# u as two more seven-product pairs in a hybrid decoder block on one core

## The chip, the cores and the metric

The kernel runs on one core of a Trainium2 chip. The metric is the device time of one execution in microseconds (us). The core has five engines with instruction queues of their own: PE (TensorE, matrix products into PSUM), DVE (VectorE), ACT (ScalarE), POOL (GpSimd, here small vector work and a queue of DMAs) and SP (SyncE, here only a queue of DMAs). Every queue runs in order: an instruction that waits for a semaphore holds back all that stand behind it on that engine.

## What is computed

The whole is one decoder block on 1024 tokens of width 1024 in float32. The part that matters here is the first half:

```python
h = _rmsnorm(x, g_mix_pre[l])
proj = jnp.einsum('bsd,de->bse', h, w_in[l]) + b_in[l]
u_pool, q, k, v, gates = jnp.split(proj, IN_SPLITS, axis=-1)   # 512, 512, 128, 128, 2048 columns
y_pool = _multiscale_pool(u_pool, w_pool[l], pool_scale[l])
...
y_attn = _sliding_window_sink_attention(q, k, v, attn_sinks[l])
g = jax.nn.sigmoid(gates)
g_pool, g_attn = g[..., :D_MODEL], g[..., D_MODEL:]
merged = (g_pool * jnp.einsum('bsc,cd->bsd', y_pool, w_branch_pool[l])
          + g_attn * jnp.einsum('bsc,cd->bsd', y_attn, w_branch_attn[l]))
```

The output projection, the residuals, the norms and the squared-ReLU MLP follow. Their code is not touched.

## The kernel before

Operands of float32 products are held as a high and a low part (`split`, L99: ACT casts to the high part, L101 or L103, then DVE subtracts it for the low part, L104). A product takes three matmul passes, high x high, high x low, low x high (`PASSES`). A matmul is 128 rows by 128 columns of weights against 512 columns of tokens.

**Stages of the first half.** First come q, k and v of the first four token tiles. Then the attention (L788 to L868) runs over eight tiles n of 128 tokens: transposes of the probabilities (`attend_t`, L396), masking (`attend_own`), the exponentials of the next tile (`softmax_exp`), their scaling, the product with v (`attend_v`, L420), scores of the tile after next (`score`), q and k of a later one (`post_qkv`). This is a long chain of ACT and DVE work, and PE would idle in it, so a generator `others` (L676) hands out other PE work in portions: `fill(t)` takes about t us from it. Its work is q, k, v of the later tiles, then per group gi of 128 columns u (`u_half`, L638: 24 matmuls for each half of the tokens) and the product of the pool weight with the branch weight (`wb_mm`, L659). `between` holds the operand splits that belong to it, which run at the middle of a portion.

The gates follow: 2048 columns as eight pairs of 256 columns. `Pairs` (L472) computes a 2 x 2 block product with seven half-size products of 12 matmuls each (4 blocks of the inner dimension, three passes) in place of eight, by sums of weight blocks and of input blocks. The products 1, 2, 3 read the plain inputs (`B11`, `B21`, `B22`), 4 to 7 read sums of inputs (`T1` to `T4`), which `build_gate` (L766) makes from x, loaded once more. Products 1 and 2 of all eight pairs run first (`first`, `second`), with the input sums built beside them. Their result `f0` stays in SBUF for six pairs and is spilled to DRAM for two. Then a loop over the pairs p does the rest: weights loaded (`load`), their sums and splits (`operand`), products 6, 4 and 3 of the pair before, 5, 7. The results are scaled with the norm (`rb`), pass a sigmoid and go to DRAM (`gate_close*`).

Last, the attention's output is fetched (`load_attn`, L933: two loads per quarter, added by DVE at L942, then split) and eight branches follow, each with 24 matmuls for the attention half (`branch`, L981). Among them stand the four pooling steps (`pool_part`, L990), which load u, add shifted copies and split.

**Order.** Inside `tc.manual_schedule` blocks the program's own order holds for the named engines. Elsewhere a scheduler orders the instructions at build time. Tiles come from pools with a fixed number of buffers (`st` 3, `wp` 6, `ga` 6, `yy` 4, `xp` 16, `gp` 17; PSUM: 2 x 2 banks `sc` and 4 `mm` in the attention, 4 `at` and 4 `mm` after), and a new tile waits until its buffer is free.

Of the kernel before, what the change touches and what calls it, by code (L numbers as in the profile page):

```python
# [14 lines left out]
P = 128  # L15
# [35 lines left out]
def block_kernel(ctx: ExitStack, tc, xt, x, consts, vecs, sinks, b_qkv, g_post, g_mlp, g_mlp_post,  # L51
# [344 lines left out]
    def attend_t(n):  # L396

        s8 = scores.pop(n)
        pt = [at("s4", 4, [NH, P], F32R) for _ in range(2)]
        bs = bank("sc", [2, 4, P])  # L400
        for kv in range(2):
            for m in range(4):
                pe.transpose(bs[:, kv, m], s8[:, kv, m], ident)  # L403
# [68 lines left out]
    class Pairs:  # L472
# [15 lines left out]
        def operand(self, p, i):  # L488
# [20 lines left out]
            self.w[p, i] = t  # L509
# [7 lines left out]
        def mm(self, b, p, i, kts=range(4), after=False):  # L517
            w, xo = self.w[p, i], self.X[OPERAND[i]]
            for kt in kts:
                for j, (wh, xh) in enumerate(PASSES):  # L520
                    x_ = xo[kt][xh] if isinstance(xo[kt], tuple) else xo[kt][:, xh, :]
                    pe.matmul(b, w[:, wh, kt, :], x_, start=not after and kt == 0 and j == 0,  # L522
                              stop=kt == 3 and j == 2, skip_group_check=after)
# [84 lines left out]
    between, hurry, due = ([], []), [False], ([], [])  # L608
# [8 lines left out]
    def load_u(gi):  # L617
        ws = stage([NK, P])
        nc.sync.dma_start(ws, w_u[gi])

        def parts():
            wu[gi] = wslot([NK, P]), wslot([NK, P])
            split(*wu[gi], ws)
        between[1].append(parts)

    def load_wb(gi):
# [9 lines left out]
        between[0].append(parts)  # L636

    def u_half(gi, th):  # L638

        if th == 0:  # L640
            ut[gi] = ga_.tile([P, S], F32, tag="ga", name=nm("u"))
        (whi, wlo), u = wu[gi], ut[gi]
        sl = slice(th * 512, (th + 1) * 512)
        b = bank("mm")

        mms = [(k, xh, 0) for k in range(NK) for xh in range(2)] + [(k, 0, 1) for k in range(NK)]
        for j, (k, xh, h) in enumerate(mms):
            pe.matmul(b, (whi, wlo)[h][:, k, :], xr(k, xh, th), start=j == 0, stop=j == len(mms) - 1)  # L648
            if j == 7 and hurry[0]:
                due[th].append(lambda: flush(between[th]))  # L650
            elif j == 7:
                flush(between[th])
            if j % 2:
                yield 2 * 0.227
        dve.tensor_tensor(u[:, sl], b, rb[:, sl], ALU.mult)
        if th == 1:
            nc.sync.dma_start(u_dram[gi], u)
# [16 lines left out]
    ut, wpts = {}, []  # L674

    def others():  # L676
        for n in range(4, NT):
            bq[n] = bank("mm")
            for k in range(NK):
                mm_q(n, k, bq[n])  # L680
                if n == NT - 1 and k == 3:
                    flush(between[1])
# [3 lines left out]
            if n == 5:  # L686
                load_u(3)
# [7 lines left out]
        for gi in (3, 2, 1, 0):  # L695
            load_wb(gi)
            if gi:
                load_u(gi - 1)
            yield from u_half(gi, 0)
            yield from u_half(gi, 1)  # L700
            yield from wb_mm(gi)
# [13 lines left out]
    def pool_in(gi, u, place):  # L715
# [4 lines left out]
        while step < w:  # L720
# [3 lines left out]
            src, step = t, 2 * step  # L724
        dve.scalar_tensor_tensor(u[:, w - 1:], src[:, w - 1:], 1.0 / w, u[:, w - 1:], ALU.mult, ALU.subtract)
        dve.tensor_tensor(src[:, :w - 1], src[:, :w - 1], cst[:, C_CNT:C_CNT + w - 1], ALU.mult)
        dve.tensor_tensor(u[:, :w - 1], src[:, :w - 1], u[:, :w - 1], ALU.subtract)

# [4 lines left out]
    def gate_first(f, b):  # L733
        dve.tensor_tensor(f, b, rb[:, :512], ALU.mult)

    def gate_close(m, f):
        act.activation(f, f, AF.Sigmoid, bias=vec[:, V_BG + m:V_BG + m + 1])
        nc.scalar.dma_start(z_dram[m], f)

    def gate_close0(m, f):  # L740
        dve.tensor_tensor(f[:, 512:], f[:, 512:], rb[:, 512:], ALU.mult)
        gate_close(m, f)

    def gate_close1(m, f):
        dve.tensor_tensor(f, f, rb, ALU.mult)
        gate_close(m, f)

    def gate_close_third(m, f, b):
        dve.tensor_tensor(f[:, 512:], f[:, 512:], rb[:, 512:], ALU.mult)
        dve.tensor_tensor(f[:, :512], b, rb[:, :512], ALU.mult)  # L750
# [5 lines left out]
    gt = Pairs(w_g, ar, gate_result, gate_first, gate_close0, gate_close1, gate_close_third)  # L756
# [9 lines left out]
    def build_gate(kt, place):  # L766

        ab = raw_x.pop(kt)
        act.activation(ab[0], ab[0], AF.Identity, scale=vec[:, V_G + kt:V_G + kt + 1])
        gb = vec[:, V_G + 4 + kt:V_G + 5 + kt]  # L770
        a0, a1, b0, b1 = (t[:, th * 512:(th + 1) * 512] for t in ab for th in range(2))
# [4 lines left out]
        yield  # L776
        for name, src in (("T2", b1), ("T1", a0), ("T3", a1), ("T4", b0)):
            t = place()
            split(t[:, 0, :], t[:, 1, :], src)
            gt.X[name][kt] = t  # L780
        yield
# [6 lines left out]
    with tc.manual_schedule(engines={mybir.EngineType.PE, mybir.EngineType.DVE, mybir.EngineType.Activation}):  # L788
# [39 lines left out]
        for n in range(NT):  # L828
# [3 lines left out]
            if n + 1 < NT:  # L832
                softmax_exp(n + 1, range(8))
            if n + 1 < NT:
                softmax_scale(n + 1)
                fill(5.0 if n == 1 else 4.4)
# [3 lines left out]
            else:  # L840
                fill(4.0)
                gt.prepare(0)
# [3 lines left out]
            if n == 6:  # L846
                load_x(0, lambda: at("qkv", 3, [S]))
# [9 lines left out]
            if n + 3 < NT:  # L857
                post_qkv(n + 3)
            if n + 2 < NT:
                softmax_max(n + 2)  # L860
        gt.prepare(1)
# [3 lines left out]
        gt.prepare(2)  # L865
        load_x(1, lambda: ga_.tile([P, S], F32, tag="ga", name=nm("xr")))
        for _ in build_gate(0, lambda: xp.tile([P, 2, 512], F32R, tag="x", name=nm("T"))):
            pass  # L868
# [17 lines left out]
    NG0, NHELD = 8, 6  # L886

    def first(p):
        gt.m1(p, bank("mm"), g32([S]) if 2 <= p < NHELD else None)

    def second(p):
        gt.m2(p)
        if p >= NHELD:
            nc.scalar.dma_start(z_dram[2 * p], gt.f0.pop(p))

    def later_builds():
        for kt in (1, 2, 3):
            yield from build_gate(kt, lambda: gr([2, 512]))

    with tc.manual_schedule(engines={mybir.EngineType.PE, mybir.EngineType.DVE, mybir.EngineType.Activation,  # L900
                                     mybir.EngineType.SP}):
        builds = later_builds()
        gt.load(6)
        gt.load(8)
        load_x(2, lambda: g32([S]))
        first(0)
        first(1)
        for p in range(NG0):
            if p + 3 < NG0:
                gt.operand(p + 3, 1)  # L910
            if p + 2 < NG0:
                first(p + 2)
            if p == 6:
                gt.operand(0, 7)
            if 1 <= p <= 6:
                next(builds)
            if p == 5:
                gt.operand(0, 6)
            second(p)
            if p + 3 < NG0:  # L920
                gt.operand(p + 3, 2)
            if p == 1:
                load_x(3, lambda: ga_.tile([P, S], F32, tag="ga", name=nm("xr")))
            if p + 5 < NG0:
                gt.load(2 * p + 10)
            elif p < 5:
                gt.load(p - 3)
            elif p == 6:
                gt.load(2)
                gt.load(3, g32([NK, P]))  # L930
    asp = [[None, None], [None, None]]

    def load_attn():  # L933
        for kh in range(2):
            for th in range(2):
                ws, wl = stage([2, 512]), stage([2, 512])
                for kv in range(2):
# [905 lines left out]
```

## Time and profile before

| what | us |
|---|---|
| median of three runs | 1105.17 (1104.57 to 1107.03) |
| the profiled execution | 1104.52 |
| its span, first to last instruction | 1102.7 |

In the page, PE, PEld (weight loads), DVE, ACT and POOL are shown with their busy time; L numbers are lines of the kernel. Matmuls are pipelined, so the mean time of one (389 ns) is longer than the step from one to the next. Names to the left and right of `<-` are the tiles written and read, numbers left out: `wh` is a weight operand of `wp`, `st` a staging tile, `s` a tile of scores or probabilities, `sc` a PSUM bank of the attention, `z` and `g` results of the gates, `ya` the attention's output, `d` u in the pooling, `qr` a tile onto which POOL's DMA adds.

### The profile page before, as it was taken

To read this page: it belongs to the slowest core of one execution; us is meant where nothing else is said; L and a number is where in the kernel's file an instruction comes from. 1 tells how busy PE (TensorE), PEld (TensorE's weight loads), DVE (VectorE), ACT (ScalarE), POOL (GpSimd) and SP (SyncE) were. 2 spreads that over 40 slices of the span, in tenths; PEclk is the share of its full clock that TensorE was granted. 3 is DMA by queue.
4 is the path that set the end of the run, shared out by engine and by line. 5 is a ranking of instruction groups with operands and counts; after the bars stand their busy time and mean duration, and the time that the engine had idled before them with its cause. 6 is when DMAs were issued, how large, how long until landed. Compare 5 with 4: busy or idle time off the path is not lost.

```text
span 1102.7 us, 13828 instructions
## 1 busy us (share of the span) xinstructions
PE 1093.7 (99%) x5114; PEld 908.5 (82%) x5114; DVE 788.6 (72%) x1125; ACT 582.4 (53%) x977; POOL 54.2 (5%) x112
## 2 busy tenths in 40 slices
PE   9999999999999999999999999999999999999997
PEld 8888888888888888888888888888888888888886
DVE  6568877897669797988867756564647875447797
ACT  7556665564432237566666555555436535435462
POOL 0334100000000001100000000000000000000000
PEclk9999999999999999999999999999999999999999
DMA  9614466365876566932455544435697875332652
GB/s 338 173 40 153 150 180 243 135 211 188 232 286 212 170 175 139 294 112 99 176 190 206 200 149 158 152 134 216 245 352 267 300 269 191 96 95 75 219 187 93
DMA packets 90803, 206.86 MB, mean 188 GB/s; under 512 B 9328, under 2 KB 22256, under 8 KB 90736
## 3 DMA queue, kind: packets, MB, share of 16 engines
q1 hardware_dynamic: 81072, 176.75, 47.5%
q10 hardware_dynamic: 5760, 19.79, 4.6%
q0 software_dynamic: 3904, 9.44, 3.9%
q8 instruction: 40, 0.66, 0.2%
q14 instruction: 27, 0.22, 0.1%
HBM read 149.32 MB, written 55.58 MB: 186 GB/s over the span
## 4 chain that ended last, share of the span: by engine, by line
PE 96%; DVE 2%; ACT 1%; issue 0%; DVEq 0%; ACTq 0%
PE mm L522 23%; PE at L522 17%; PE at L1611 15%; PE mm L1611 12%; PE mm L456 5%; PE mm L1146 5%; PE mm L648 3%; PE mm L458 3%; PE mm L192 2%; PE sc L183 2%; PE mm L183 2%; PE at L1146 2%; PE sc L429 1%; PE sc L360 1%; PE at L1192 1%; PE sc L403 1%
## 5 line engine op out<-in xcount | busy, mean ns | idle before, releaser
L1611 PE MATMUL at<-ar,wh 128*128 128x512 f32 x696 | 158.7, 389 | 0.0
L1611 PEld LDWEIGHTS at<-ar,wh 128*128 128x128 f32 x696 | 130.6, 188 | 27.1
L1611 PE MATMUL mm<-ar,wh 128*128 128x512 f32 x576 | 131.0, 389 | 0.0
L1611 PEld LDWEIGHTS mm<-ar,wh 128*128 128x128 f32 x576 | 108.1, 188 | 22.5
L104 DVE TENSOR_TENSOR wh<-raw,wh 128x1024 fp32r<-128x1024 f32 x51 | 62.3, 1222 | 78.3 <-ACT wh L101 78.3
L101 ACT CAST wh<-raw 128x1024 fp32r<-128x1024 f32 x51 | 53.7, 1053 | 115.0 <-PE at L1611 55.5
L104 DVE TENSOR_TENSOR wh<-st,wh 128x512 fp32r<-128x512 f32 (+1 forms) x105 | 74.3, 718 | 26.1 <-ACT wh L101 21.7
L101 ACT CAST wh<-st 128x512 fp32r<-128x512 f32 (+1 forms) x104 | 65.7, 642 | 41.3 <-PE mm L456 14.9
L522 PE MATMUL mm<-T,wx 128*128 128x512 f32 x348 | 82.8, 389 | 0.0
L522 PEld LDWEIGHTS mm<-T,wx 128*128 128x128 f32 x348 | 65.3, 188 | 13.6
L522 PE MATMUL mm<-T,wh 128*128 128x512 f32 x240 | 58.9, 389 | 0.0
L522 PE MATMUL at<-gr,wh 128*128 128x512 f32 x243 | 58.8, 390 | 0.0
L522 PE MATMUL mm<-gr,wh 128*128 128x512 f32 x240 | 57.2, 391 | 0.0
L522 PEld LDWEIGHTS at<-gr,wh 128*128 128x128 f32 x243 | 45.5, 188 | 10.0 <-DVE gr L104 0.5
L522 PEld LDWEIGHTS mm<-T,wh 128*128 128x128 f32 x240 | 45.0, 188 | 9.7 <-DVE z L586 0.4
L522 PEld LDWEIGHTS mm<-gr,wh 128*128 128x128 f32 x240 | 44.7, 188 | 9.1
L648 PE MATMUL mm<-x,wh 128*128 128x512 f32 x192 | 47.7, 395 | 0.0
L104 DVE TENSOR_TENSOR ar<-B,ar 128x1024 fp32r<-128x1024 f32 x37 | 45.1, 1220 | 2.0 <-ACT ar L101 1.9
L522 PE MATMUL at<-ar,wh 128*128 128x512 f32 x192 | 46.1, 389 | 0.0
L522 PE MATMUL at<-T,wx 128*128 128x512 f32 x192 | 46.1, 389 | 0.0
L522 PE MATMUL mm<-x,wh 128*128 128x512 f32 x192 | 43.7, 389 | 0.0
L522 PEld LDWEIGHTS at<-T,wx 128*128 128x128 f32 x192 | 36.0, 188 | 7.5
(429 smaller groups left out, 2178.0 us busy)
## 6 DMA issues: line engine op xcount, KB each, us to landing
raw<-f_dram SPq DMA_DIRECT2D x53, 512.0 KB, 3.8
f_dram<-g SPq DMA_DIRECT2D x28, 512.0 KB, 3.3
st<-in_w_up_dram SPq DMA_DIRECT2D x24, 512.0 KB, 4.4
B<-in_w_dn_dram SPq DMA_DIRECT2D x24, 512.0 KB, 6.9
st<-in_w_g_dram SPq DMA_DIRECT2D x18, 512.0 KB, 4.3
f_dram<-g ACTq DMA_DIRECT2D x17, 512.0 KB, 2.9
g<-spill_dram SPq DMA_DIRECT2D x16, 512.0 KB, 5.0
raw<-in_w_dn_dram SPq DMA_DIRECT2D x16, 512.0 KB, 4.6
```

The source lines that it names most:

```text
L101: act.copy(hi, src)
L104: eng.tensor_tensor(lo, src, f32(hi), ALU.subtract)
L183: pe.matmul(bq, xs_[k][n // 4][:, xh, n % 4 * P:(n % 4 + 1) * P], wq[k][:, h, :], start=k == 0 and j == 0, stop=k == NK - 1 and j == 2)
L192: pe.matmul(bkv_of(n), xs_[k][n // 4][:, xh, n % 4 * P:(n % 4 + 1) * P], wkv[k // 2][:, h, k % 2, :], start=k == 0 and j == 0 and not (joi ...
L360: pe.matmul(sb[:, kv, i, :nk], qt[r, qx, m * P:(m + 1) * P], kx[r, k0:k0 + nk], start=j == 0, stop=j == 2)
L403: pe.transpose(bs[:, kv, m], s8[:, kv, m], ident)
L456: pe.matmul(bs[th], whi[:, k, :], rhs(k, hl, th), start=k == 0 and hl == 0, stop=False)
L458: pe.matmul(bs[th], wlo[:, k, :], rhs(k, 0, th), start=False, stop=k == nk - 1)
L522: pe.matmul(b, w[:, wh, kt, :], x_, start=not after and kt == 0 and j == 0, stop=kt == 3 and j == 2, skip_group_check=after)
L648: pe.matmul(b, (whi, wlo)[h][:, k, :], xr(k, xh, th), start=j == 0, stop=j == len(mms) - 1)
L1146: pe.matmul(bs[t], Am[a][k][ah][:, t * P:(t + 1) * P], Wm[w][k][wh], start=not after and k == 0 and j == 0, stop=k == 3 and j == 2, skip_g ...
L1611: pe.matmul(bs[t], fo[fh][:, k2, t * P:(t + 1) * P], wo_[wh][:, k2, :], start=not after and s2 == 0 and k2 == 0 and j == 0, stop=(s2, k2) ...
```

## The change

u becomes pairs 8 and 9 of `Pairs`: its weights are appended to those of the gates, and each pair takes seven products. The generator now fills the attention with products 1 and 2 of eight pairs (8, 9, 0 to 5) through `half`, which spills both results to DRAM, ACT copying them out of PSUM. Products 1 and 2 of pairs 6 and 7 come after the attention. Products 4 to 7 of pairs 8 and 9 run side by side in eight PSUM banks, one block of the inner dimension at a time, so that each block of the input sums is needed only when its turn comes. For the other pairs the spilled result is reloaded and a DMA of POOL's queue adds product 1 onto product 2 (`load_f0`). Weight operands are split two products at a time (`both`), input sums likewise (`split_gate`). The probabilities are split as one piece of 128 x 1024. The attention's halves are loaded by SP and added by POOL's DMAs (`attn_load`), earlier than before. Two of the four pooling steps start inside the pair loop. The scaling with `rb` moves to the end of each result.

```diff
-        for kv in range(2):
-            split(*(t[:, 4 * kv:4 * kv + 4] for t in pt), bs[:, kv])
+        split(*(flat(t) for t in pt), bs.rearrange("p a b k -> p (a b k)"))
...
+        def both(self, p, i, j, src, tile_):
+
+            hi, lo = tile_([2, 4, P]), tile_([2, 4, P])
+            split(hi, lo, src)
+            self.w[p, i], self.w[p, j] = (hi[:, 0], lo[:, 0]), (hi[:, 1], lo[:, 1])
...
-    def u_half(gi, th):
...
+    def half(p, i):
+
+        if i == 1:
+            gt.f0[p] = ga_.tile([P, S], F32, tag="ga", name=nm("f0"))
+        f, b = gt.f0[p], bank("mm")
+        for kt in range(4):
+            gt.mm(b, p, i, (kt,))
...
+            yield 3 * 0.227
+        act.copy(f[:, 512:] if i == 1 else f[:, :512], b)
+        if i == 2:
+            nc.sync.dma_start(f_spill(p), gt.f0.pop(p))
...
             if n + 1 < NT:
-                softmax_exp(n + 1, range(8))
-            if n + 1 < NT:
+                early = 1.0 if n > 2 else 0.0
+                softmax_exp(n + 1, range(4))
+                fill(early)
+                softmax_exp(n + 1, range(4, 8))
                 softmax_scale(n + 1)
...
+    def load_f0(p):
+        f = gt.f0[p] = ga_.tile([P, S], F32, tag="ga", name=nm("f0")) if 1 <= p <= 3 else g32([S])
+        nc.sync.dma_start(f, f_spill(p))
+        if p not in (6, 7):
+            nc.gpsimd.dma_start(f[:, :512], f_spill(p)[:, 512:], accum_op=ALU.add)
...
+        for kt in range(4):
+            for (p, i), b in late_banks.items():
+                gt.mm(b, p, i, (kt,))
+            if kt < 2:
+                sum_gate(kt + 2)
+                split_gate(kt + 2, lambda: gr([2, 512]))
...
+        for p in range(1, 7):
+            load_f0(p + 1)
+            load_pair_of(p + 1)
...
+            act.copy(f1[:, V], b)
+            dve.tensor_tensor(f1[:, V], f1[:, V], e, ALU.add)
+            gt.mm(c, p, 6, after=True)
+            gt.sums56(p + 1)
+            gt.sums37(p + 1)
+            act.copy(gt.f0[p][:, V], c)
+            gt.split56(p + 1, xp_tile if p < 6 else ar)
+            gt.mm(b, p - 1, 4, after=True)
+            act.copy(f1[:, U], b)
+            dve.tensor_tensor(f1, f1, rb, ALU.mult)
+            gt.operand(p, 4)
+            gt.mm(e, p - 1, 3, after=True)
+            if p < 6:
+                gt.start(p + 1, bank("mm"))
+            dve.tensor_tensor(f0[:, V], f0[:, V], e, ALU.add)
+            gate_sigmoid(2 * p - 1, f1)
+            dve.tensor_tensor(f0, f0, rb, ALU.mult)
+            gt.split37(p + 1, wslot)
+            gate_sigmoid(2 * p - 2, f0)
+            gt.m5(p, bank("at"))
+            gt.mm(c, p, 7, after=True)
...
-                dve.tensor_tensor(ws, ws, wl, ALU.add)
...
+    def attn_load(th, kh):
+        ws = attn_raw[th, kh] = stage([2, 512])
+        for i, q in enumerate((nc.sync, nc.gpsimd)):
+            for kv in range(2):
...
+                q.dma_start(ws[kv * HD:(kv + 1) * HD], src[:, r:r + HD].rearrange("m p q -> p m q"),
+                            **({"accum_op": ALU.add} if i else {}))
```

More of the change, by code (lines that the diff above doesn't have):

```diff
@@ L635, in parts @@
             dve.scalar_tensor_tensor(lo, ws, sc, f32(hi), ALU.mult, ALU.subtract)
-        between[0].append(parts)
-    def u_half(gi, th):
[L640 to L657, printed above, removed]
+        (lazy if gi > 1 else between[0]).append(parts)
     def wb_mm(gi):
@@ L948, in block_kernel @@
[L948 to L973 removed]
+        gt.load(19, g32([NK, P]))
@@ L976, in gate_load @@
+    f1 = gate_result()
+    act.copy(f1[:, V], gt.chain[6])
+    dve.tensor_tensor(f1[:, V], f1[:, V], gt.fifth[6], ALU.add)
+    gt.f1[6] = f1
+    gt.operand(7, 4)
+    b6 = bank("at")
+    gt.mm(b6, 7, 6)
+    gt.m4(6)
+    gt.m3(6)
+    gt.rest(7, gate_result(), b6, bank("mm"), bank("at"), done=(6,), then=attn_splits)
     def gate_load(m):
```

354 lines of the change are left out of this document (218 added, 136 removed).

## The prediction

> **What bounds the kernel now.** I read the page's first part and its chain of waits, then the list of who waited for whom on PE, then busy time by stretch.
>
> ```profile
> span 1102.7 us, 13828 instructions
> PE 1093.7 (99%) x5114; PEld 908.5 (82%) x5114; DVE 788.6 (72%) x1125; ACT 582.4 (53%) x977; POOL 54.2 (5%) x112
> ...
> PE 96%; DVE 2%; ACT 1%; issue 0%; DVEq 0%; ACTq 0%
> ```
>
> ```profile
> PE mm L201 <- DVE pad L160: 1.1, 1, 1.1
> PE sc L403 <- DVE s L369: 0.5, 1, 0.5
> ```
>
> ```profile
> 85.00:162.00 77.00, 76.47 (x452) 63.45 (x451) 63.95 (x93) 49.84 (x139) 14.37 (x30) 1.00 0.53 159
> 162.00:205.00 43.00, 43.00 (x192) 35.60 (x191) 33.42 (x52) 22.84 (x39) 0.00 (x0) 1.00 0.60 218
> 402.00:483.00 81.00, 81.00 (x375) 67.42 (x374) 65.83 (x99) 52.98 (x96) 12.97 (x14) 1.00 0.65 182
> 1080.00:1103.00 23.00, 15.31 (x74) 12.68 (x72) 15.93 (x39) 4.60 (x15) 0.00 (x0) 0.91 0.25 92
> ```
>
> The chain is 96% PE, and PE waited twice: 1.1 us at the start, 0.5 us in the attention. The columns of the stretches are length, busy time (and instructions) of PE, PE's weight loads, DVE, ACT and POOL, the clock, the DMA share and GB/s. What PE loses lies in the last stretch (7.7 us), which the change does not touch. So a matmul less is worth its whole time, and any wait newly put on PE costs its whole time. A busy PE need not run at its peak, so I take its rate from the chain's pieces:
>
> ```profile
> 88.98 5.93 PE mm L648 x26
> 97.63 1.64 PE sc L360 x24
> 225.15 8.16 PE mm L522 x36
> ```
>
> ```profile
> L648 PE MATMUL mm<-x,wh 128*128 128x512 f32 x192 | 47.7, 395 | 0.0
> ```
>
> L522 (all seven-product work) runs at 8.16/36 = 0.2267 us a matmul, L648 (u) at 5.93/26 = 0.228. A product, 12 matmuls, is 2.72 us.
>
> **Removed from PE.** u now takes 4 column groups x 2 halves x 24 = 192 matmuls, the count of the last row. As two pairs it takes 2 x 7 x 12 = 168. 24 x 0.2267 = 5.4 us less, on the path. The other matmuls keep their number; in the built order the tail from the pool projection on is the same on every engine.
>
> **The attention.** PE's filling there stays at 192 matmuls (products 1 and 2 of eight pairs in place of u), but what the other engines do for it changes.
>
> ```profile
> L386 ACT ACTIVATE s<-s,nmx 128x128 f32<-128x128 f32 x40 | 15.5, 390 | 0.0
> L101 ACT CAST s<-sc 128x512 fp32r<-128x512 f32 x12 | 7.0, 587 | 16.3 <-DVE s L104 10.6 <-PE sc L403 2.4 <-issue 2.4
> L431 ACT COPY yt<-sc 128x1024 f32<-128x1024 f32 x6 | 6.1, 1012 | 4.9 <-PE sc L429 4.9
> L362 ACT COPY s<-sc 128x512 f32<-128x512 f32 x10 | 5.8, 585 | 4.4 <-PE sc L360 3.8
> L634 ACT ACTIVATE wh<-st,vec 128x1024 fp32r<-128x1024 f32 x4 | 4.6, 1150 | 0.0
> L101 ACT CAST qt<-mm 128x512 fp32r<-128x512 f32 x4 | 2.4, 588 | 1.8 <-PE mm L316 1.8
> L101 ACT CAST khi<-mm 128x128 fp32r<-128x128 f32 x4 | 1.1, 272 | 0.0
> ```
>
> ```profile
> L101 ACT CAST wh<-st 128x512 fp32r<-128x512 f32 x25 | 15.0, 619 | 9.0 <-DMA st<-in_w_g_dram 3.6 <-DVE st L504 2.0 <-DMA st<-in_w_ba_dram 1.5
> L737 ACT ACTIVATE z<-z,vec 128x1024 f32<-128x1024 f32 x10 | 11.5, 1154 | 11.7 <-DVE z L750 10.0 <-DVE z L741 1.7
> L101 ACT CAST yahi<-st 128x1024 fp32r<-128x1024 f32 x4 | 4.2, 1053 | 7.0 <-DVE st L942 7.0
> L551 ACT COPY z<-mm 128x512 f32<-128x512 f32 x6 | 3.5, 586 | 7.3 <-PE mm L522 7.3
> L104 DVE TENSOR_TENSOR wh<-st,wh 128x512 fp32r<-128x512 f32 x26 | 17.3, 686 | 2.8 <-ACT wh L101 2.7
> L942 DVE TENSOR_TENSOR st<-st,st 128x1024 f32<-128x1024 f32 x4 | 4.9, 1224 | 7.5 <-DMA st<-spill_dram 7.5
> L104 DVE TENSOR_TENSOR yalo<-st,yahi 128x1024 fp32r<-128x1024 f32 x4 | 4.9, 1218 | 0.0
> L655 DVE TENSOR_TENSOR u<-mm,rb_all 128x512 f32<-128x512 f32 x1 | 0.7, 682 | 0.0
> L773 DVE SCALAR_TENSOR_TENSOR xr<-xr,vec,xr 128x512 f32<-128x512 f32 x2 | 1.5, 752 | 0.1
> ```
>
> ACT gains 16 evacuations from PSUM at 0.586 (9.4 us; u's eight were DVE's, 0.68 each, L655). Weight casts were four of 128x1024 (1.05) and six of 128x512 (0.62) by the stage's end and become twenty of 0.62: +4.5. The probabilities' sixteen casts of 0.587 become eight of about 1.01 (L431, the same shape out of PSUM): -1.3. ACT rises by 12.6 us, from 49.8 to 62.4 of 77. DVE: -5.4 for u's scalings, +4.7 for the weights' low parts, -1.2 for the probabilities in one piece, +2.7 for the first sums of pair 8: about even.
>
> An iteration lasts about 12.8 us (transposes at 87.95 and 100.76 in the timeline below). ACT's work in one will be 1.01 + 1.01 + 1.17 + 0.59 + 0.27 + 8 x 0.39 for the attention itself, three casts and three evacuations 3.6, and 1.15 for a pool weight: 11.9. That is 93%, so its order decides.
>
> ```profile
> 87.95 1.04 PE L403 MATMUL sc<-cst,s 128*128 128x128 f32 x8
> 90.91 0.17 DVE L378 TENSOR_TENSOR es<-snk,nmx 128x8 f32<-128x8 f32 x1
> 92.30 0.39 ACT L386 ACTIVATE s<-s,nmx 128x128 f32<-128x128 f32 x1
> 100.76 1.04 PE L403 MATMUL sc<-cst,s 128*128 128x128 f32 x8
> 111.77 1.35 DVE L635 SCALAR_TENSOR_TENSOR wh<-st,vec,wh 128x1024 fp32r<-128x1024 f32 x1 [0.36 <-ACT wh L634]
> 113.81 1.09 PE L403 MATMUL sc<-cst,s 128*128 128x128 f32 x8 [0.53 <-DVE s L369]
> ```
>
> Today ACT casts half of the probabilities, then waits for DVE before it casts the other (10.6 us over 12 casts, 1.8 an iteration), with the exponentials queued behind: they begin 3.3 us after the transposes end (92.3 against 89.0). In one piece that wait goes; the exponentials then hang on DVE's row maximum alone, whose last step (L378) ends at 91.1, and begin at about +2.4. This pays for 0.9 of the 2.1 us that each of six iterations gains. The rest must fit ahead of the copy of the attention's output, which frees the PSUM bank that the second score group needs. From +2.4, 3.1 of exponentials, 1.15, two casts and two evacuations (2.4) bring ACT to +9.0; PE finishes that output at about +7.3 (24 filling matmuls and its own 8) and wants the bank back at about +9.4 (six more and the first score group, half of L360's 1.64); the copy lasts 1.0, so up to 0.6 us is lost where a pool weight falls in, and nothing elsewhere, where 1.15 is missing. What waits behind ACT is the score copy, DVE's copy of the mask from the same banks (L369) and the next transposes: the wait that cost 0.53 above. Bounds: -0.5, if today's stall goes, to +7.8, if all of ACT's waits for PE stay (0.8, 0.9 and 0.5 an iteration by the rows of L431, L362 and L101 qt: 11.9 + 2.2 = 14.1 against 12.8, six times, 7.8). I take +0.5 net, near the lower end, since DVE, the releaser in the only stall there is, gets no more to do.
>
> **The block before the pair loop.** PE runs products 1 and 2 of pairs 6 and 7, product 3 of pairs 8 and 9, then eight products side by side, one quarter of each at a time: 14 x 2.72 = 38.1 us. Each quarter (5.4 us) needs one more set of input sums, which costs DVE 0.69 + 3 x 0.75 + 2 x 1.22 = 5.4. DVE begins with pair 9's sums, whose load of w_u stands in the built order behind a store that waits for ACT's last copy of the attention, some 1.5 us into the block. With 4.7 us to land (a load's row below) DVE starts at about 6; sums 2.7, two low parts 2.4, two of 128x512 1.4 and the first 5.4 bring it to 18, the next quarters to 23 and 29, against PE's need at 21.8, 27.2 and 32.6. The inputs, 9.3 us from issue (below), are there at 11, before their turn. 4 us of slack: 0, with +3 as the other end if the loads come 7 us late. The stretch now has 218 GB/s at 0.60 of the DMA engines, so it can carry more.
>
> **The pair loop.** A pass is five products, 13.6 us. DVE in it: seven of 128x512 (4.8) and four of 128x1024 (4.9), 9.7, with 1.2 to 2.8 added (the closing of pairs 8 and 9, pool steps): 12.5 at most. ACT: three copies 1.76, a cast 0.62, the start 0.59, two casts 2.1, two sigmoids 2.3: 7.4. Weights are built a pass ahead. Only the entry is tight: DVE must free eight banks (ten adds, 6.9 us) while it prepares pair 1; worked forward it is 0 to 0.3 us late for the first product 4. +0.2, ends 0 and +1.
>
> **DMAs.** SP's list grows by twelve (twenty more of 512 KB, most of them spills and reloads of products 1 and 2, and eight fewer of the attention's 256 KB), POOL's by sixteen adds of 256 KB: eight onto the reloaded spills, read only a pass later, and eight for the attention's halves, in place of four DVE adds (4.9 us, L942).
>
> ```profile
> qr<-in_w_o_dram POOLq DMA_DIRECT2D x8, 512.0 KB, 5.9
> st<-spill_dram SPq DMA_DIRECT2D x16, 256.0 KB, 4.7
> xr<-in_xt_dram SPq DMA_DIRECT2D x4, 512.0 KB, 9.3
> c<-c POOLq DMA_DIRECT2D x4, 256.0 KB, 9.5
> ...
> 402.14 1.21 POOL L1057 DMA_DIRECT2D qr<-in_w_o_dram  x1 [40.52 <-DMA qr<-in_w_o_dram]
> ```
>
> The added wait that matters is the fourth quarter of the attention. There are three staging buffers; it gets one when DVE has split the first quarter, which stands behind an add that needs pair 7's product 6 (2.7 us after the loop) and some 5.5 us of other DVE work: +8.3. Load 4.7, two issues on POOL of 1.2, landing 5.9 after the second: +20.1. Cast 1.05, subtraction 1.22: +22.4. PE wants it after seven products and 14 matmuls of the first branch: 19.0 + 3.2 = 22.2, its low part at 22.4. Ends: 0 if half the bytes land sooner, +3.8 with 9.5 us instead of 5.9. I take +0.5. Behind this cast on ACT wait a sigmoid and the next branch's weights, needed 2.3 us later.
>
> **Sum.** The profiled execution took 1104.5 us, its span and 1.8 around it. 1104.5 - 5.4 + 0.5 + 0 + 0.2 + 0.5 = 1100.3. The median of the runs shown is 0.65 above that execution: 1100.9.
>
> **Rivals.** (1) ACT does not fit the attention and half of the upper bound is lost, 0.65 us in each of six iterations: 3.9 in place of 0.5, 1104.3, no change. For it: 93%. Against: the wait of 10.6 us that goes. (2) POOL's transfers land late: +3.8 at the branch in place of 0.5, 1104.2. For it: the row of 9.5. Against: that row writes from SBUF to SBUF, the new ones read DRAM as the 5.9 does. [...] (3) Slower: in the pair loop DVE becomes the bound. It waits for ACT five times a pass; today such a wait is 2.7 us over 26 (0.1 each). Were each as long as ACT's instruction (1.05, 1.05, 0.62, 0.59, 0.59, 3.9 in all), a pass would take 9.7 + 1.9 + 3.9 = 15.5, 1.9 over PE's 13.6, and six 11.4: 1112.1. It decides above 13.6, and slower than 0.2% from 14.7 on. Against: ACT is busy for 7.4 of 13.6, and its casts can run while DVE adds.
>
> **How the numbers follow.** 0.2% (2.2 us) is what a measurement here can tell from no change. Forecast 0.67, (1) 0.14, (2) 0.11, (3) 0.08. The forecast's own range is 1099.2 (no stall, today's gone: 1104.5 - 5.4 - 0.5 + 0.65) to 1102.9. Half of (2) and a quarter of (1) lie below 1103.0, and 0.01 is for both together with more: faster 0.76, same 0.15, slower 0.09. The range goes to 1105.0, which takes in (1) and (2), and down to 1098.9.
>
> **What would show it.** Matmul records down by 24; the chain still 96% PE or more. In the list of PE's waits: nothing over 1 us between the attention and the branches. ACT's idle time before the casts of s out of sc down from 10.6 us to about what PE causes. The fourth quarter's low part done within a microsecond of the first branch's third weight block. I am wrong if PE's waits, together with gaps in its chain, come to more than 3 us, or if L403 or L360 wait in most iterations.

## The result, and the profile after

| | before | after |
|---|---|---|
| median, us (six runs each) | 1105.48 (1103.86 to 1107.03) | 1111.26 (1109.26 to 1112.90) |
| profiled execution, us | 1104.5 | 1112.9 |
| its span, us | 1102.7 | 1111.1 |

The ratio after to before is 1.0054, with a 95% interval of 1.0040 to 1.0068: the change makes the kernel 5.8 us slower. The prediction was 1100.9 us, with a range to 1105.0. The sign was wrong. The profiled execution is the slowest of its six, 1.6 us above their median.

First the page of the kernel after: engines, and the chain's shares.

```profile
span 1111.1 us, 13837 instructions
PE 1091.8 (98%) x5090; PEld 904.8 (81%) x5090; DVE 795.5 (72%) x1094; ACT 593.7 (53%) x976; POOL 68.4 (6%) x128
...
PE 88%; DMA 4%; DVE 4%; ACT 2%; issue 1%; DVEq 0%; POOL 0%; ACTq 0%; POOLq 0%
```

The matmul records are down by 24, as forecast, and PE is busy for 1.9 us less. But PE's share of the chain fell from 96% to 88%: transfers and VectorE set the end in places. The list of PE's waits (engine, line, what it waited for: us in all, times, longest) says where:

```profile
PE at L544 <- DVE z L612: 8.0, 1, 8.0
PE mm L544 <- DVE gr L104: 1.2, 1, 1.2
PE mm L201 <- DVE pad L160: 1.1, 1, 1.1
PE at L1756 <- DVE hold L104: 0.6, 1, 0.6
```

One wait of 8.0 us is larger than all that the 24 matmuls were worth. Stretches of the kernel after (columns as in the prediction):

```profile
208.00:295.00 87.00, 87.00 (x385) 71.89 (x384) 70.45 (x87) 43.29 (x56) 7.45 (x8) 1.00 0.74 225
295.00:325.00 30.00, 21.77 (x87) 17.05 (x86) 18.57 (x24) 14.24 (x17) 3.87 (x4) 0.89 0.97 265
```

The pair loop has no gap on PE. The loss lies behind it, at pair 7, with the DMA engines at 0.97 and the clock at 0.89. Finer stretches:

```profile
268.00:282.00 14.00, 14.00 (x64) 11.58 (x63) 12.44 (x18) 8.25 (x11) 1.97 (x2) 1.00 0.80 208
282.00:295.00 13.00, 13.00 (x59) 10.63 (x57) 7.17 (x9) 4.14 (x6) 0.00 (x0) 1.00 0.26 82
295.00:317.00 22.00, 14.44 (x62) 11.10 (x60) 12.79 (x18) 8.08 (x10) 3.87 (x4) 0.94 0.98 245
```

Just ahead of the crowded stretch the DMA engines stand almost still for 13 us (0.26). What was to be loaded was not short of bandwidth (82 GB/s there, 245 in the 22 us behind it); it was not yet allowed to start. The chain through that place, in order of time (start, length, what):

```profile
282.31 5.40 DMA g<-in_w_g_dram
...
296.67 5.75 DMA st<-spill_dram
...
303.06 0.59 POOL st L1034
...
304.24 10.40 DMA st<-spill_dram
...
314.72 1.05 ACT yahi L101
...
316.94 0.69 DVE z L612
...
317.67 4.56 PE at L544 x12
```

And VectorE's timeline (start, length, instruction, in brackets the idle time before it and what ended it):

```profile
287.73 0.69 DVE L519 TENSOR_TENSOR ws<-g 128x512 f32<-128x512 f32 x1 [5.83 <-DMA g<-in_w_g_dram]
...
295.41 1.23 DVE L104 TENSOR_TENSOR wh<-st,wh 128x1024 fp32r<-128x1024 f32 x1 [0.21 <-ACT wh L101]
...
301.16 2.35 DVE L104 TENSOR_TENSOR yalo<-st,yahi 128x1024 fp32r<-128x1024 f32 x2
...
315.80 1.23 DVE L104 TENSOR_TENSOR yalo<-st,yahi 128x1024 fp32r<-128x1024 f32 x1 [8.81 <-ACT yahi L101]
316.94 0.68 DVE L612 TENSOR_TENSOR z<-z,at 128x512 f32<-128x512 f32 x1
```

Read backwards: PE's last product of pair 7 is summed onto product 5 in the same bank, and L612 has to read product 5 there first. L612 is queued on VectorE behind the low part of the *third* attention quarter (315.80). That waits for ScalarE's cast, the cast for POOL's second adding transfer (issued at 304.24, landed 10.4 us later), that for the plain load, and the load started at 296.67 because only then was a staging buffer free: the split of pair 7's weights (295.41) had just released it. The two other buffers held the first two quarters, loaded since 235.8 and 264.2 (SP's issues) and split only at 301.16. Ahead of it all VectorE stood 5.8 us for pair 7's weights, whose tile came free at 282.3 with the landing of a result's store.

By the start of the stage after the branches (the first matmul of L1146 before, L1291 after) the kernel is 6.7 us late: 402.47 against 409.15. From there to the end it took 700.2 us before and 702.0 after; in the kernels below this part took between 700.2 and 704.9 us (experiment 2 the longest), though none of them changes anything there. Why is not known, and every whole time carries this spread.

### The profile page after: what moved, and what is told of

Its sections match the earlier page's. It is cut to its first block, busy times and chain, and to the rows that moved or that the text cites. A ratio compares the mean times of both kernels' runs of the same rounds, so it can differ in the third digit from the quotient of the medians.

```text
span 1111.1 us, 13837 instructions
## 1 busy us (share of the span) xinstructions
PE 1091.8 (98%) x5090; PEld 904.8 (81%) x5090; DVE 795.5 (72%) x1094; ACT 593.7 (53%) x976; POOL 68.4 (6%) x128
## 4 chain that ended last, share of the span: by engine, by line
PE 88%; DMA 4%; DVE 4%; ACT 2%; issue 1%; DVEq 0%; POOL 0%; ACTq 0%; POOLq 0%
PE mm L544 24%; PE at L544 16%; PE at L1756 11%; PE mm L1756 11%; PE mm L455 5%; PE mm L1291 5%; PE mm L457 3%; PE sc L183 2%; PE mm L192 2%; PE mm L183 2%; PE at L1291 2%; DMA st<-spill_dram 1%; PE sc L428 1%; PE sc L360 1%; DMA raw<-in_w_dn_dram 1%
## 5 line engine op out<-in xcount | busy, mean ns | idle before, releaser
L544 PE MATMUL mm<-T,wx 128*128 128x512 f32 x372 | 89.5, 389 | 0.0
L544 PEld LDWEIGHTS mm<-T,wx 128*128 128x128 f32 x372 | 69.8, 188 | 14.5
L544 PE MATMUL mm<-gr,wh 128*128 128x512 f32 x321 | 77.5, 391 | 1.2 <-DVE gr L104 1.2
L544 PEld LDWEIGHTS mm<-gr,wh 128*128 128x128 f32 x321 | 59.8, 188 | 13.8 <-DVE gr L104 1.6
L544 PE MATMUL mm<-T,wh 128*128 128x512 f32 x267 | 66.3, 390 | 0.3 <-ACT wh L101 0.2
L544 PEld LDWEIGHTS mm<-T,wh 128*128 128x128 f32 x267 | 50.0, 188 | 11.4 <-ACT wh L101 0.6
L544 PE MATMUL mm<-x,wh 128*128 128x512 f32 x240 | 58.8, 394 | 0.0
L544 PE MATMUL at<-T,wx 128*128 128x512 f32 x213 | 52.0, 389 | 0.0
L544 PEld LDWEIGHTS mm<-x,wh 128*128 128x128 f32 x240 | 44.2, 188 | 9.5 <-ACT f L653 0.2
L544 PEld LDWEIGHTS at<-T,wx 128*128 128x128 f32 x213 | 40.0, 188 | 8.3
```

The source lines that it names most:

```text
L544: pe.matmul(b, w[wh][:, kt, :], x_, start=not after and kt == 0 and j == 0, stop=kt == 3 and j == 2, skip_group_check=after)
```

## Experiments

Theory A was that the queue place alone is the loss. The rivals were that the data are late wherever the split stands (B), that the loss is elsewhere (C), and that the adding transfer is at fault (D). All medians are compared with runs of the kernel before on the same chip (1104.7 to 1105.0 us; 1105.5 beside the kernel after), so a difference between two changed kernels is uncertain by the 0.8 us between those.

**1. The split behind the add.**

```diff
     def attn_splits():
         attn_load(*ORDER[3])
-        for o in ORDER[2:]:
-            attn_split(*o)
...
     gt.rest(7, gate_result(), b6, bank("mm"), bank("at"), done=(6,), then=attn_splits)
+    for o in ORDER[2:]:
+        attn_split(*o)
```

> The changed kernel, with the split of the third attention quarter put behind pair 7's add of product 5 on VectorE (both last quarters are split after pair 7's calls). Theory A (the queue place is the loss: the data would be in time for the branch): the 8.0 us wait at L544 and the 1.8 us of slower matmuls behind it go, nothing over 1 us comes in their place, 1101 to 1103 us. Theory B (the data itself are late, wherever the split stands): the low part of the fourth quarter still comes at about 322 us of the span, when PE asks for it at about 315.5 (the last product from 309.7, 2.7 us, then 14 matmuls of the first branch), so a wait of 5 to 7 us appears at the first branch and the time is 1107 to 1110 us. Theory C (the loss lies in the attention or the second half, not here): 1109 to 1111 us, with the wait gone.

Measured 1109.64 us (ratio 1.0046, 1.0031 to 1.0061). The wait at L612 is gone, and PE waits elsewhere:

```profile
PE mm L455 <- ACT wh L101: 6.3, 1, 6.3
PE mm L455 <- DVE t L748: 1.6, 1, 1.6
```

ScalarE casts the first branch's weights behind the third quarter's high part, for which it stood 13.0 us. The second row is the fourth quarter: its low part ends just ahead of L748 on VectorE, at 324.4 us. A falls and B has the time right, though most of the wait is the third quarter's, where B named the fourth's: another queue place hands the same lateness to another instruction.

**2. Two loads and a VectorE add** for the last two quarters, as in the kernel before.

```diff
+    def attn_load2(th, kh):
+        ws = attn_raw[th, kh] = stage([2, 512])
+        wl = stage([2, 512])
...
+        dve.tensor_tensor(ws, ws, wl, ALU.add)
...
         for o in ORDER[2:]:
+            attn_load2(*o)
             attn_split(*o)
```

> The changed kernel, with the last two attention quarters loaded as before: two staging buffers each, all four transfers on SP's queue and the halves added by VectorE. Theory A (place) sees the split still queued on VectorE beside pair 7's adds; in the built order the add of product 5 now stands ahead, so it expects 1101 to 1104 us. Theory B (late data): four buffers out of three for two quarters, so the fourth quarter starts later than now; it expects a wait of 4 to 10 us at the first branch, 1106 to 1113 us. Theory D (it is the adding transfer on POOL's queue, 10.4 us from issue to landing, that makes the data late): without it the third quarter is there some 8 us sooner, and the time is 1102 to 1105 us although the staging is no better.

Measured 1115.03 us: the time that D forecast is missed, and it lies above even B's end. D's mechanism is not excluded by that, for the third quarter's cast starts at 309.04 us in place of 314.72:

```profile
309.04 1.05 ACT L101 CAST yahi<-st 128x1024 fp32r<-128x1024 f32 x1 [2.54 <-DVE st L1045]
```

But the edit takes two buffers for each quarter, and PE now waits 7.5 us at the first branch, for weights whose load had to wait for a staging buffer in its turn. The stage after the branches starts at 407.0 us, 2.1 ahead of the kernel after, so what makes the whole slower than that kernel lies behind it, and why is not shown.

**3. Other tiles for the last two quarters.**

```diff
-        ws = attn_raw[th, kh] = stage([2, 512])
+        ws = attn_raw[th, kh] = yy.tile([P, 2, 512], F32, tag="y", name=nm("ya")) if kh else stage([2, 512])
```

(with both loads issued at the end of the last pass)

> The changed kernel, with the last two attention quarters loaded into two tiles of the pool y that stand free in the pair loop, so both loads are issued by the end of the sixth pass without waiting for a staging buffer. Theories A, B and D alike: both quarters are there before pair 7's adds, the 8.0 us wait goes and nothing replaces it: 1100.5 to 1103 us, 8 to 10.5 below the changed kernel and 3 to 5 below the kernel before. Theory C (the loss lies elsewhere): 1108 us or more.

Measured 1111.04 us, no gain, against all of A, B and D. But C, which had that time, is no better: the wait is still there, in a new place. The pool y also holds the results of pairs 6 and 7, and with two of its four tiles taken a result waits for a store to land. From this kernel with the sums of experiment 4, which waits in the same place (5.6 us; 4.9 in experiment 3), PE's list and ScalarE's timeline:

```profile
PE mm L544 <- ACT z L1108: 5.6, 1, 5.6
```

```profile
300.71 0.59 ACT L1108 COPY z<-mm 128x512 f32<-128x512 f32 x1 [5.71 <-DMA spill_dram<-z]
```

**4. The same, with the block's sums moved.** In the block before the pair loop, the second quarter's input sums go ahead of a split into a tile that is still being spilled. In the kernel after, VectorE's row of that split is:

```profile
178.66 1.23 DVE L104 TENSOR_TENSOR ar<-ws,ar 128x1024 fp32r<-128x1024 f32 x1 [1.86 <-DMA spill_dram<-f]
```

```diff
-        gt.split56(9, ar)
-        gt.operand(8, 4)
         scale_gate(1)
+        sum_gate(1)
+        gt.split56(9, ar)
+        gt.operand(8, 4)
...
         gt.mm(b3[8], 8, 3)
-        sum_gate(1)
```

> The same as the kernel with the early staging, and in the block before the pair loop the second quarter's input sums are put ahead of pair 9's split on VectorE, which waits for a tile that is still being spilled. The 1.2 us wait of PE at L544 for the input's low part goes: 1.0 to 1.5 us below the kernel with the early staging alone, 1099.5 to 1102 us. If that wait only hid a later one of the same length (pair 9's operands then come 1.2 us late), the two kernels are within 0.5 us.

Measured 1109.52 us, 1.5 below experiment 3, and the wait of 1.2 us is gone: a cause of its own, worth about what it showed (the ranges of the two kernels overlap; in the profiled executions it is 1.1 us by the stage after the branches). The time itself misses the expectation with experiment 3.

So a new theory was needed: a chain of buffers (E), which begins where pair 7's weights wait for their tile; against it, too many bytes for this stretch (F).

**5. Pair 7's second weights in a tile that matmuls free.**

```diff
         gt.load(2 * p)
-        gt.load(2 * p + 1, xp.tile([P, NK, P], F32, tag="x", name=nm("r1")) if p < 6 and p % 2 == 0 else g32([NK, P]))
+        gt.load(2 * p + 1, xp.tile([P, NK, P], F32, tag="x", name=nm("r1")) if p % 2 == 0 and p < 6 or p == 7 else g32([NK, P]))
```

> The changed kernel, with the second half of pair 7's weights loaded into a tile of the pool xp, which matmuls free, in place of one of the pool g, which a result's store frees. Theory E (the chain begins there: in the changed kernel this load is issued at 282.3 us, when the store of the result of 277.4 has landed, VectorE stands for 5.8 us at pair 7's weight sums, and all that is queued behind them, the attention's splits and with them the staging buffers, is late by that): the sums begin at about 283 instead of 287.7, limited by the other half's load, so everything behind is 4 to 5 us earlier and the wait of 8.0 falls to 0 to 3.5 us; 1102 to 1107 us. Theory F (the transfers of this stretch are simply too many bytes, 0.97 of the DMA engines from 295 to 325): the same bytes move, the wait stays above 6 us, 1109 to 1111.5 us.

Measured 1112.07 us (1110.32 to 1114.40), above the ranges of both theories. The sums do start earlier (282.4 us), and the median wins nothing. The first two quarters are still split late (299.7), so the fourth quarter's buffer, and the load and adds behind it, stay late; PE waits 3.3 us at the third quarter's split and 0.8 at the fourth's, in the profiled execution, which is the fastest of the four. The chain's piece that decides is the fourth's second add:

```profile
308.16 12.44 DMA st<-spill_dram
...
320.68 1.06 ACT yahi L101
```

**6. The first two quarters split first,** in the 5.8 us in which VectorE stands idle for pair 7's weights.

```diff
+            if p == 6:
+                attn_split(*ORDER[0])
+                attn_split(*ORDER[1])
             gt.sums56(p + 1)
...
-        attn_split(*ORDER[0])
-        attn_split(*ORDER[1])
```

> The changed kernel, with the splits of the first two attention quarters moved ahead of pair 7's weight sums in the last pass, into the 5.8 us in which VectorE stands idle for those weights. Theory E: two staging buffers come free at about 284 and 286 instead of 302, the third and fourth quarters are loaded in the stretch from 282 to 295 in which the DMA engines are at 0.26, and are added by 302; no wait at pair 7's adds or at the branch; pair 7's weights are as late as before, which costs PE nothing or up to 1 us: 1100.5 to 1104 us. Theory F: the same bytes, the wait only moves; 1107 us or more.

Measured 1104.37 us (1101.80 to 1107.42, ten runs), 0.4 above E's range and 6.9 below the changed kernel with the same bytes moved and pair 7's weights as late as ever (VectorE's row of 287.04). VectorE and SP in this kernel:

```profile
282.21 2.35 DVE L104 TENSOR_TENSOR yalo<-st,yahi 128x1024 fp32r<-128x1024 f32 x2
287.04 0.69 DVE L519 TENSOR_TENSOR ws<-g 128x512 f32<-128x512 f32 x1 [2.48 <-DMA g<-in_w_g_dram]
```

```profile
283.86 2.96 SPq L1034 DMA_DIRECT2D st<-spill_dram  x4
```

Both last quarters are loaded from 283.9 on, where the changed kernel loads one at 296.7 and the other at 302.4. F falls. With experiment 5 this turns E into theory G: what decides is not the weights' tile but the staging buffers, two of three held by quarters that were loaded two passes ahead and not split.

**7. Both, and the sums of experiment 4.**

> Both edits together (pair 7's second weights in a tile of xp, the first two quarters split ahead of pair 7's sums), and the second quarter's input sums ahead of pair 9's split. Theory E: nothing over 1 us is left in PE's waits between the attention and the branches; the forecast's own sum comes back: 1099 to 1102.5 us, 2.5 to 5.5 below the kernel before. Theory F: 1106 us or more. If PE still waits there, another tile or queue place is next in the chain.

Measured 1100.15 us (1099.61 to 1100.25; ratio 0.9954, 0.9939 to 0.9969): 4.9 us faster than the kernel before and 11.1 faster than the changed one. PE has no gap in this stretch, and the transfers fill the hole:

```profile
282.00:295.00 13.00, 13.00 (x60) 10.74 (x59) 9.59 (x12) 7.46 (x9) 3.87 (x4) 1.00 0.97 240
295.00:317.00 22.00, 22.00 (x99) 18.22 (x98) 17.58 (x24) 11.37 (x13) 0.00 (x0) 1.00 0.88 291
```

**8. One part alone: the probabilities in one piece,** in the kernel before (the first lines of the change's diff, and nothing else).

> The kernel before, with only the probabilities split in one piece. If the forecast's reading of the attention is right (ScalarE's 10.6 us of waiting for VectorE between the two casts goes, and with it PE's one wait there of 0.5 us): 0 to 0.8 us below the kernel before. If the one longer cast makes the exponentials or the score copy later (rival): 0.5 to 3 us above it, with waits at L403 or L360.

Measured 1104.69 us (ratio 1.0003, 0.9994 to 1.0012), nothing that can be measured. PE's wait for L369 is still there, at 0.4 us.

**9. One part alone: the halves added by transfers,** in the kernel before.

```diff
-                ws, wl = stage([2, 512]), stage([2, 512])
+                ws = stage([2, 512])
...
+                    nc.gpsimd.dma_start(ws[kv * HD:(kv + 1) * HD], src[:, r:r + HD].rearrange("m p q -> p m q"), accum_op=ALU.add)
...
-                dve.tensor_tensor(ws, ws, wl, ALU.add)
```

> The kernel before, with only the attention's halves added by transfers on POOL's queue (one staging buffer a quarter in place of two, four adds of VectorE less). Theory G (what is late is the quarters' chain of staging buffer, load, two adding transfers, cast and subtraction, and VectorE's queue behind it): in the kernel before the last split ends at 308.8 us, 1.2 us before pair 7's add of product 7 (310.0) is wanted, so an adding transfer of 6 to 10 us in each quarter's chain makes it late by 1 to 8 us, 1106 to 1113 us. Rival (one buffer in place of two lets all quarters start sooner, which pays for the slower adding): 1103.5 to 1105.5 us, and then the adding transfers were not at fault in the changed kernel.

Measured 1112.90 us (ratio 1.0069, 1.0052 to 1.0086), 8.0 us slower from this part alone, at the upper end; in the profiled executions the loss is 6.9 us by the stage after the branches (409.39 against 402.47). PE waits for ScalarE, in whose queue a cast stands for an adding transfer of 9.8 us (the chain at 278.86), with the copy that empties PE's bank behind it:

```profile
PE mm L522 <- ACT z L551: 5.4, 2, 3.5
```

```profile
288.74 1.04 ACT L101 CAST yahi<-st 128x1024 fp32r<-128x1024 f32 x1 [5.95 <-DMA st<-spill_dram]
289.69 0.58 ACT L551 COPY z<-mm 128x512 f32<-128x512 f32 x1
```

In the kernel before, no such cast stands directly ahead of L551. The order here is the scheduler's, and it changed with the edit, so the 8.0 us hold the slower adding and the new place in the queue together.

**10. The same part taken back from the good kernel:** experiment 7 with the two loads of experiment 2.

> The kernel with both edits and the early sums (1100.15 us), with its last two quarters loaded as two halves each on SP's queue and added by VectorE. Theory G: with the staging buffers free at 281 us either way is in time; within 1.5 us of that kernel, 1099 to 1102 us. If the adding transfers cost anything by themselves (they take POOL's queue and hold the DMA engines longer): 0.5 to 2 us less than that kernel. If two buffers a quarter are again too few: a wait at pair 7 or the first branch, 1103 us or more.

Measured 1103.50 us (1100.99 to 1104.89), 3.4 us above experiment 7, with several waits of 0.5 and 0.6 us. That is the time of the third case, and SP's timeline bears it out:

```profile
294.44 2.57 SPq L1044 DMA_DIRECT2D st<-spill_dram  x4
```

With two buffers each, the fourth quarter's load starts only here, where experiment 7 starts those of both last quarters from 280.36 us on. Not all of the 3.4 us need be the edit's: by the attention's last output product, ahead of anything that it changes, this profiled execution is already 1.4 us behind that of experiment 7. So the adding transfers lose 8.0 us in experiment 9, where quarters queue for their buffers just ahead of their use, and are no worse than the two loads where the buffers are free early. What they cost by themselves, apart from the buffers, is not shown.

**11 and 12. What a wait costs PE.** In experiment 7's kernel, VectorE work of a known length ahead of one add in the third pass, with no transfer late.

```diff
+            for _ in range(10 if p == 3 else 0):
+                dve.tensor_tensor(f1[:, V], f1[:, V], f1[:, V], ALU.max)
             dve.tensor_tensor(f1[:, V], f1[:, V], e, ALU.add)
```

(eighteen in place of ten in the second kernel)

> The kernel with both edits and the early sums, with ten more VectorE instructions of 0.6 us (the larger of a tile and itself, which changes nothing) ahead of the add of product 5 in the third pass of the pair loop. The add ends 3.9 us before PE wants the bank, so PE should wait 2.0 to 2.5 us there, with no transfer late. If PE's granted clock falls after any wait of more than 2 us: 1.5 to 2.5 us more in the matmuls behind it, 1103.5 to 1105 us. If it falls only after longer ones: 1102 to 1103 us and a clock of 1.00 behind the wait.

> The same with eighteen such instructions: PE should wait 6.5 to 7.5 us for VectorE, with no transfer late. If the slow matmuls after the 8.0 us wait come from the wait itself, the next dozen takes 4 to 5 us in place of 2.72 here too, at a granted clock of about 0.5, and the time is 1107.5 to 1110 us. If they came from the crowded DMA engines there, the clock stays at 1.00 and the time is 1106 to 1107.5 us.

One instruction of the chain took 0.73 us, not 0.6, so the waits came out at 3.3 and 9.1 us, longer than expected, and with them both medians above every range: 1107.23 (1103.88 to 1109.17) and 1114.20 us (two runs). PE after the wait of 9.1 us, and the stretches of 4 us around it:

```profile
252.38 5.41 PE L544 MATMUL at<-x,wh 128*128 128x512 f32 x12 [9.11 <-DVE z L1077]
257.62 0.84 PE L544 MATMUL at<-T,wx 128*128 128x512 f32 x3
```

```profile
248.00:252.00 4.00, 0.00 (x0) 0.00 (x0) 3.76 (x6) 0.00 (x0) 0.00 (x0) 0.50 0.60 169
252.00:256.00 4.00, 3.62 (x9) 2.85 (x10) 3.93 (x6) 2.31 (x4) 0.92 (x1) 0.50 0.39 66
256.00:260.00 4.00, 4.00 (x16) 3.27 (x15) 3.81 (x6) 2.54 (x4) 0.00 (x0) 0.80 0.26 58
```

Twelve matmuls take 5.24 us (257.62 - 252.38) in place of 2.72, at a clock of 0.50 and with the DMA engines at 0.39. In experiment 7 the clock stays at 1.00 with the DMA engines at 0.97. So the slow matmuls came from the wait here, not from the transfers. What stays open is the spread of the kernel with the 3.3 us wait: its profiled execution, the fastest of eight, is 3.6 us above that of experiment 7 (6.1 later at the stage after the branches, 2.4 quicker from there on), its median 7.1 us.

## Why the prediction was wrong, step by step

- **24 matmuls fewer, -5.4.** Right. The records show 24 fewer, and experiment 7, where no new wait is left, starts the stage after the branches at 395.86 against 402.47, 6.6 us ahead; 0.5 of that is a start that came sooner (first transposes at 62.62 against 63.12), and some 1 us beyond the sum is not accounted for.
- **Attention, +0.5 within -0.5 and +7.8.** Right: from the first transposes to the start of the last output product it took 95.32 us before and 95.61 after, +0.3. ScalarE did fit, with 62.9 us busy from 85 to 162 us where 62.4 were forecast, and its casts no longer wait for VectorE (10.6 us before). The second row is a term that the step left out:

```profile
L101 ACT CAST s<-sc 128x1024 fp32r<-128x1024 f32 x6 | 6.1, 1020 | 2.6 <-issue 1.2 <-ACT khi L101 0.8 <-ACT wh L665 0.5
L386 ACT ACTIVATION_READ_ACCUMULATOR s<-s,nmx 128x1 f32 x40 | 7.5, 188 | 0.0
```

  Rival (1) is out. The sum for one iteration (11.9 of 12.8 us) lacked the read-outs that follow the exponentials, eight of 0.19 us; with them its fullest iteration has 13.4, more than there was room for (the 62.4, which start from the measured 49.8, have them). That the stage lost only 0.3 us all the same was in part luck. Experiment 8 shows that the one piece alone gains nothing, so the end at -0.5 was not to be had.
- **Block before the pair loop, 0 within 0 and +3.** Low by 1.2 us, inside its bounds. The loads of inputs and weights were in time; what was missed is a split queued ahead of the sums, into a tile whose 512 KB store took 7.1 us to land (experiment 4).
- **Entry of the pair loop, +0.2, and rival (3), VectorE as its bound.** PE is busy for 87.00 of 87.00 us: nothing lost, rival (3) is out.
- **The fourth quarter, +0.5 within 0 and +3.8. This step failed,** in three ways. First, it asked only when the branch wants the *fourth* quarter. The *third* is split on VectorE ahead of L612, for which PE comes six products after the loop; the step named what stands behind the cast on ScalarE and did not ask the same of VectorE, where the low part stands ahead of pair 7's add. Second, it took durations from quiet rows. Counted from the loop's end (309.7, when PE asks, less six products: 293.4) the fourth's buffer comes at +9.0 (302.4) against the +8.3 of the step, but its cast starts at 319.83, +26.4, where the step had +20.1. The rows of the transfers' issues on POOL's timeline:

```profile
303.06 0.97 POOL L1034 DMA_DIRECT2D st<-spill_dram  x1 [31.67 <-DMA st<-spill_dram]
304.24 0.96 POOL L1034 DMA_DIRECT2D st<-spill_dram  x1 [0.20 <-issue]
311.25 0.96 POOL L1034 DMA_DIRECT2D st<-spill_dram  x1 [6.05 <-DMA st<-spill_dram]
312.86 0.97 POOL L1034 DMA_DIRECT2D st<-spill_dram  x1 [0.64 <-DMA st<-spill_dram]
```

  The load from 302.41 on lands 8.7 us after issue (median of its two transfers) and not 4.7. The third quarter's adds land 9.5 and 10.4 us after issue and not 5.9; the fourth's, issued last, land after 6.1 and 5.8, as the step had it, and the cast then stands 1.2 us behind other work of ScalarE. So PE waits even without L612, and by more than the step's end of +3.8: in experiment 1 it waits 6.3 us for weights whose cast stands behind the third quarter's, and 1.6 for the fourth's low part. Third, a wait was priced at its length. The 8.0 us cost 9.8: the twelve matmuls behind it took 4.56 in place of 2.72.
- **Rival (2), transfers on POOL land late.** Its mechanism was the nearest to what happened, at 3.8 in place of 9.8 us; experiment 9 has that part, alone in the kernel before and with the order that the scheduler then chose, at 8.0. It was not the issue that was slow: POOL's four issues above took 0.96 to 0.97 us each, the first two with VectorE at work and the last two with it idle.
- **The sum.** At that stage the kernel after is 6.7 us late. The terms found are -5.4 + 8.0 + 1.8 + 1.2 + 0.3 = 5.9; of the other 0.8, 0.2 is a later start of the attention (63.31 against 63.12) and the rest is not accounted for. With the three edits of experiment 7, none of which touches what the change is for, the measured 1100.15 us is 0.8 from the forecast. That it is so near is in part luck: by the stage after the branches that kernel had gained 6.6 us where the sum had 4.2, and from there on it took 702.6 us in place of 700.2, which the sum left unchanged. The change was worth about what the sum said; the order and the buffers that came with it were not looked at closely enough.

## What to carry to other kernels

When a transfer is moved ahead, ask how long its buffer is then held and who else draws from that pool: here two quarters loaded two passes early held two of three staging buffers until a late place in VectorE's queue, and the loads behind them missed 13 us of idle DMA engines. Follow every split, cast or add of late data on *each* in-order queue and name what stands directly behind it; here, taking the wait of 8.0 us out of VectorE's queue only handed it to ScalarE's (6.3 us in experiment 1), until the buffer was freed earlier. And price a load in a stretch by how crowded it will be (8.7 us here, with the DMA engines at 0.98), not by the median of the whole kernel (4.7).

## What the runs showed of the hardware that was not expected

**The matmuls behind the longer waits were slower.** Behind the shorter wait of experiment 9 (1.9 us) the next twelve matmuls took 2.85 us, where twelve take 2.72 in a row without a wait; over the kernel after's wait of 1.2 us the granted clock was 1.00 (184 to 187 us). Behind longer ones the next twelve took 5.26 us (a wait of 3.3, experiment 5), 4.11 (3.5, experiment 9), 5.28 (5.6, experiment 4) and 5.24 (9.1, experiment 12, at a clock of 0.50). In the kernel after, around its 8.0 us wait:

```profile
312.00:316.00 4.00, 0.00 (x0) 0.00 (x0) 0.20 (x1) 1.28 (x2) 1.19 (x2) 0.77 0.97 165
316.00:320.00 4.00, 2.33 (x6) 1.85 (x7) 3.31 (x5) 3.60 (x5) 0.00 (x0) 0.50 0.79 192
320.00:324.00 4.00, 4.00 (x17) 3.26 (x16) 2.47 (x3) 3.38 (x4) 0.00 (x0) 0.87 1.05 389
```

The clock was 0.50 from 316 to 320 us. The price was 1.8 us there by the chain's piece (4.56 - 2.72), or 1.7 from start to start (4.40 - 2.72), and 2.5 us after the wait of 9.1 us (5.24 - 2.72). PE's lists have no wait between 1.9 and 3.3 us, so how long a wait has to be for this is not shown.

**The adding transfers held the DMA engines longer.** From 300 to 316 us, the kernel after's transfers by queue, with MB and share of 16 engines' time:

```profile
q1 hardware_dynamic: 1040, 2.67, 62.9%
q0 software_dynamic: 480, 0.89, 34.8%
```

The second row is POOL's queue, which carried only adding transfers there: 6.3 us of all 16 engines per MB (0.348 x 16 us / 0.89) against 3.8 for the first row's plain ones (0.629 x 16 / 2.67), 1.7 times as much. Part of that was the size of the packets: POOL's were of 2 KB, the plain row's of 2 and 4 KB (137 and 223 ns each). Among packets of 2 KB alone, the kept trace has 203 ns each for POOL's queue and 137 for the plain one in the same 16 us, 1.5 times as much.
